# Feature-major products: the high and low parts of x side by side, one matmul of 512 columns for both

## The chip, the core and the metric

One core of a Trainium2 chip runs the whole program once. TensorE (PE) multiplies a stationary tile, loaded by a weight load (PEld), with a moving tile and adds into PSUM; VectorE (DVE), ScalarE (ACT) and GpSimd (POOL) do the element-wise work; SyncE (SP) issues most transfers. Each engine works through its own instructions in the order of the program; semaphores make it wait for the others. The metric is the device time of one execution in microseconds (us), a median over runs.

## What is computed

Two networks in a row on 256 tokens of 1024 features, all in float32. The first has two layers of pooling mixer, stick-breaking attention and a feed-forward part, which is dense SwiGLU in layer 0 and eight experts in layer 1. The second has two layers of a gated recurrence (hgrn), three groups of dilated window attention and a squared-ReLU feed-forward part. Cut to the products that the change touches:

```python
# first block, per layer
proj = h @ w_in[layer]                        # q and k of the stick-breaking attention are columns of proj
f = (silu(h @ ffn_wg) * (h @ ffn_wu)) @ ffn_wd        # layer 0: 2816 hidden columns
# second block, per layer
z = rms_norm(x, norm1_g) @ w_in_2             # zq, zf of the recurrence; q, k of three attention groups
x = x + jnp.square(jax.nn.relu(h2 @ w_up)) @ w_down   # 4096 hidden columns
```

## The kernel before

**Products in three terms.** A float32 operand is kept as a high part (rounded to the type that TensorE multiplies in one pass) and a low part (the rest). x @ w is made of three products, high x high, low x high and high x low, added up in PSUM. `mm3` (line 213) issues the three.

**The weight stream.** Weights come in units of 1 MB, `raw` [128, 2048], loaded by SP. `emit_split` (line 149) makes the high part `whi` on ACT (line 162) and the low part `wlo` on DVE (line 164). All of `raw`, `whi`, `wlo` live in one pool of 13 slots, so the making of a unit's parts can wait for PE to be done with an older unit. `take(1)` hands out the next unit and, first, splits the unit that is two further on: its two instructions stand in the queues of ACT and DVE at that place.

**Token-major products** (`tok_part`, `chunk_tok`, `down`): x is stationary, 512 columns of weights move (lines 221 to 223).

**Feature-major products** (`chunk_feat`): 512 columns of x @ w, turned, so that features lie on partitions. Here a 128 x 128 block of the weights is stationary and the 256 tokens of x move: three matmuls of 256 columns for each block (lines 217 to 219, xh on whi, xl on whi, xh on wlo). A chunk takes two units (j = 0, 1), four column tiles c of 128 features, four k tiles each: 32 triples, 96 matmuls. Two PSUM banks hold the result, two column tiles in each; the pool `acc` has four banks, so two chunks can be in flight. After every second column tile `pump()` emits a piece of the side work (attention, recurrence).

**Consumers.** After a chunk, ACT and DVE read the finished banks, 512 columns at a time: q and k of the mixer (lines 581, 583), SwiGLU in `ffn` (lines 700 to 704: Silu on ACT, product on DVE, high part on ACT, low part on DVE), the gates of the recurrence (lines 1089 to 1099), q and k of the attention groups (line 1117, ACT alone), the squared ReLU of the up-projection (lines 1172 to 1176: Relu on ACT, product on DVE, high part on ACT, low part on DVE). There are 44 chunks: 4 in the mixers, 10 in `ffn`, 16 in the attention stage of the second block, 14 in its two up-projections. `rotate` (line 1217) turns the first 32 rows of q and k on DVE (lines 1219, 1220), with a product on POOL of what a transfer (`rot`) brought.

The order on every engine is that in which the program emits its instructions; nothing reorders them.

Of the kernel before, what the change touches and what calls it, by code (L numbers as in the profile page):

```python
# [43 lines left out]
def constants():  # L44
    """Arrays that follow from the shapes alone."""
# [49 lines left out]
class Net:  # L95
# [81 lines left out]
    def filler(self, n=1):  # L177
        """Work put off to where VectorE would wait."""
# [3 lines left out]
    def ahead(self, split, dma):  # L182
        """Splits the units up to split after the next, loads those up to dma after it."""
# [44 lines left out]
    def tok_part(self, x, ws, t):  # L228
        """Token tile t of 512 columns of x @ w (8 k tiles, two units)."""
# [41 lines left out]
    def chunk_feat(self, x):  # L271
        """Feature-major 512 columns of x @ w: two banks of two 128-column tiles by 256 tokens."""
        xh, xl = x
        out = [self.bank(), self.bank()]
        for j in range(2):
            w = self.take(1)[0]
            for c in range(4):
                o = out[c // 2][:, (c % 2) * T:(c % 2 + 1) * T]
                for k in range(4):
                    kt = 4 * j + k  # L280
                    self.mm3(o, xh[:, kt, :], xl[:, kt, :], w[0][:, k, c * P:(c + 1) * P],
                             w[1][:, k, c * P:(c + 1) * P], kt == 0 and c % 2 == 0, kt == 7,
                             w_stationary=True, skip_group_check=True)
                if c % 2 == 1:
                    self.pump()
        return out

    def down(self, x, nkt, tail=2, done=None, head=None, next_head=None):
        """Token-major x @ w of 1024 columns, 2 k tiles a unit: banks [token tile][half]. The last units
        go tile by tile, and done(t) follows; with head, which makes token tile t of x, all (four)  # L290
        do, and next_head() makes token tile 0 of what comes next while the other's products run."""
# [5 lines left out]
        def part(t, js, ws):  # L297
            """Adds units js to token tile t, half by half."""
# [57 lines left out]
    def to_feat(self, dst, src, t, kt0=0, n=8):  # L356
        """Token-major src [128, n * 128] of token tile t to feature-major high and low parts."""
# [4 lines left out]
    def rstd(self, var, eps, between=None):  # L362
        """(var[0] + var[1] + eps) ** -0.5; between() follows while VectorE would wait."""
# [7 lines left out]
    def load_rows(self, aps, queue=None):  # L371
        """Rows of 1024 on all partitions."""
# [21 lines left out]
        # -mean / 32 and -mean; squares of (x - mean) / 32 add up to the variance.  # L394
# [14 lines left out]
    def rms_norm(self, dst, src, g, acc=None):  # L409
        """dst = norm(src); with acc, src grows by it first."""  # L410
# [13 lines left out]
    def run(self, stop=None):  # L424
# [4 lines left out]
        self.x = (self.main.tile([P, KT, T], F32R, name="xh"), self.main.tile([P, KT, T], F32R, name="xl"))  # L429
# [132 lines left out]
    def mixer(self, l, ps):  # L562
# [3 lines left out]
        with self.mixs:  # L566
# [12 lines left out]
            for j in range(2):  # L579
                ps = self.chunk_feat(self.x)  # L580
                nc.scalar.activation(q[:, 2 * j:2 * j + 2].rearrange("p c t -> p (c t)"), ps[0], AF.Identity,
                                     scale=0.125)
                nc.vector.tensor_copy(k[:, 2 * j:2 * j + 2].rearrange("p c t -> p (c t)"), ps[1])
# [96 lines left out]
    def ffn(self, ps):  # L680
        nc, a, tc = self.nc, self.a, self.tc
        with tc.tile_pool(name="ffn", bufs=1) as pool, tc.tile_pool(name="ffnw", bufs=2) as work:
# [13 lines left out]
            self.side.append(first())  # L696
            for j in range(1, FF // 256):
                ps2 = self.chunk_feat(self.x)
                s = work.tile([P, 512], F32, name="s")
                nc.scalar.activation(s, ps2[0], AF.Silu)  # L700
                nc.vector.tensor_mul(s, s, ps2[1])
                h, l = (m[:, 2 * j:2 * j + 2].rearrange("p c t -> p (c t)") for m in hid)
                nc.scalar.activation(h, s, AF.Identity)
# [691 lines left out]
```

## Time and profile before

| what | value |
|---|---|
| median of 3 runs | 2160.26 us (2159.03 to 2164.56) |
| span of the profiled execution | 2159.9 us |
| PE busy, PEld busy | 98%, 84% of the span |
| DVE busy, ACT busy, POOL busy | 69%, 56%, 4% |
| weights moved | 509 MB, 236 GB/s on average |

The profiled execution's only time of its own is its span; it lies 0.4 us under the median of the runs. The profile lists the busy time of each engine, rows of single instructions (start, duration, what they waited for) and groups of like instructions. Matmuls are pipelined: PE rows overlap, so the pace is the distance between two starts and not the duration in the row. A stretch of `ffn` runs from about 124 to 240 us, the two up-projections from 1513 to 1594 and 1982 to 2063 us, the attention stages from 1223 to 1460 and 1692 to 1930 us, the experts from 430 to 1195 us.

### The profile page before, as it was taken

What the parts mean: (1) busy time and instruction counts of PE and PEld (TensorE: products, weight loads), DVE (VectorE), ACT (ScalarE), POOL (GpSimd) and SP (SyncE); (2) the same over time, 40 slices, a digit from 0 to 9 for tenths busy, and PEclk for the clock granted to TensorE, in tenths of its full rate; (3) what the DMA queues carried; (4) which work ended last, traced back from release to release, by engine and by line L of the source; (5) the groups of instructions that cost most, each with busy time, mean ns of one, the idle gap of its engine ahead of it and who ended that gap; (6) DMA issues with size and microseconds to landing.
All of it is one profiled execution on the core that took longest, in us unless ns stands there. A gap on an engine that the chain in (4) does not pass through costs nothing. (4 is left out here: it accounts for less than half of the span.)

```text
span 2159.9 us, 28622 instructions
## 1 busy us (share of the span) xinstructions
PE 2112.7 (98%) x11787; PEld 1824.0 (84%) x11787; DVE 1498.4 (69%) x1327; ACT 1217.8 (56%) x1199; POOL 81.0 (4%) x91
## 2 busy tenths in 40 slices
PE   7999999999999999999999799999999999999998
PEld 6889978788888888888888599987998899988986
DVE  6465564698888989898989566666654566666643
ACT  4544345677777777777777444464543434455542
POOL 1000000000000000000000101100000011100000
PEclk9999999899999999999999899999999999999999
DMA  9275555599999999999998454444654654436551
GB/s 317 78 234 178 193 169 201 198 362 357 363 338 369 360 343 352 370 363 338 364 353 303 139 181 139 144 157 139 232 195 138 220 165 156 139 123 226 183 194 59
DMA packets 240122, 509.33 MB, mean 236 GB/s; under 512 B 9360, under 2 KB 56592, under 8 KB 239984
## 3 DMA queue, kind: packets, MB, share of 16 engines
q1 hardware_dynamic: 236448, 496.21, 66.6%
q0 software_dynamic: 3248, 10.69, 1.7%
q8 instruction: 95, 1.56, 0.3%
q10 hardware_dynamic: 288, 0.52, 0.1%
q14 instruction: 43, 0.35, 0.0%
HBM read 504.77 MB, written 1.05 MB: 234 GB/s over the span
## 5 line engine op out<-in xcount | busy, mean ns | idle before, releaser
L164 DVE TENSOR_TENSOR wlo<-raw,whi 128x2048 fp32r<-128x2048 f32 x463 | 1062.7, 2298 | 369.1 <-ACT whi L162 313.9
L162 ACT ACTIVATE whi<-raw 128x2048 fp32r<-128x2048 f32 x467 | 886.7, 1914 | 269.0 <-PE acc L222 84.6
L221 PE MATMUL acc<-whi,xh 128*128 128x512 f32 x1168 | 468.0, 401 | 3.1 <-ACT xh L346 2.1
L223 PE MATMUL acc<-whi,xl 128*128 128x512 f32 x1168 | 459.6, 393 | 0.5 <-DVE xl L347 0.5
L222 PE MATMUL acc<-wlo,xh 128*128 128x512 f32 x1168 | 457.5, 392 | 1.6 <-DVE wlo L159 1.0
L217 PE MATMUL acc<-xh,whi 128*128 128x256 f32 x1408 | 404.0, 287 | 0.0
L219 PE MATMUL acc<-xh,wlo 128*128 128x256 f32 x1408 | 398.5, 283 | 0.0
L218 PE MATMUL acc<-xl,whi 128*128 128x256 f32 x1408 | 398.3, 283 | 0.0
L221 PE MATMUL acc<-whi,hidh 128*128 128x512 f32 x696 | 275.9, 396 | 0.0
L223 PE MATMUL acc<-whi,hidl 128*128 128x512 f32 x696 | 275.0, 395 | 0.0
L222 PE MATMUL acc<-wlo,hidh 128*128 128x512 f32 x696 | 274.7, 395 | 0.0
L217 PEld LDWEIGHTS acc<-xh,whi 128*128 128x128 f32 x1408 | 270.0, 192 | 1.3
L218 PEld LDWEIGHTS acc<-xl,whi 128*128 128x128 f32 x1408 | 270.0, 192 | 0.7
L219 PEld LDWEIGHTS acc<-xh,wlo 128*128 128x128 f32 x1408 | 269.9, 192 | 0.2 <-DVE wlo L164 0.2
L223 PEld LDWEIGHTS acc<-whi,xl 128*128 128x128 f32 x1168 | 220.1, 188 | 52.5 <-DVE xl L347 5.9
L221 PEld LDWEIGHTS acc<-whi,xh 128*128 128x128 f32 x1168 | 220.8, 189 | 49.9 <-ACT xh L346 5.5
L222 PEld LDWEIGHTS acc<-wlo,xh 128*128 128x128 f32 x1168 | 221.0, 189 | 46.5 <-DVE wlo L159 1.8
L223 PEld LDWEIGHTS acc<-whi,hidl 128*128 128x128 f32 x696 | 130.9, 188 | 30.9
L222 PEld LDWEIGHTS acc<-wlo,hidh 128*128 128x128 f32 x696 | 131.0, 188 | 29.2
L221 PEld LDWEIGHTS acc<-whi,hidh 128*128 128x128 f32 x696 | 130.9, 188 | 29.1
L346 ACT ACTIVATE xh<-tr 128x512 fp32r<-128x512 f32 x40 | 22.5, 596 | 74.1 <-PE tr L353 73.9
L925 ACT ACTIVATE hidh<-tr 128x512 fp32r<-128x512 f32 (+1 forms) x48 | 27.1, 564 | 64.7 <-PE tr L353 64.7
(305 smaller groups left out, 1603.6 us busy)
## 6 DMA issues: line engine op xcount, KB each, us to landing
raw<-in_moe_wd_dram SPq DMA_DIRECT2D x88, 1024.0 KB, 6.5
raw<-in_moe_wg_dram SPq DMA_DIRECT2D x80, 1024.0 KB, 6.2
raw<-in_moe_wu_dram SPq DMA_DIRECT2D x80, 1024.0 KB, 6.3
raw<-in_w_in_dram SPq DMA_DIRECT2D x74, 1024.0 KB, 5.4
raw<-in_w_up_dram SPq DMA_DIRECT2D x32, 1024.0 KB, 5.4
raw<-in_w_down_dram SPq DMA_DIRECT2D x32, 1024.0 KB, 5.0
raw<-in_w_out_dram SPq DMA_DIRECT2D x16, 1024.0 KB, 5.5
raw<-in_ffn_wg_dram SPq DMA_DIRECT2D x22, 512.0 KB, 4.2
```

The source lines that it names most:

```text
L162: self.nc.scalar.activation(hi, raw, AF.Identity)
L164: self.nc.vector.tensor_sub(lo, raw, hi.bitcast(F32))
L217: mm(out, wh, xh, start=start, stop=False, **kw)
L218: mm(out, wh, xl, start=False, stop=False, **kw)
L219: mm(out, wl, xh, start=False, stop=stop, **kw)
L221: mm(out, xh, wh, start=start, stop=False, **kw)
L222: mm(out, xh, wl, start=False, stop=False, **kw)
L223: mm(out, xl, wh, start=False, stop=stop, **kw)
L346: self.nc.scalar.activation(h, v, AF.Identity)
L925: nc.scalar.activation(h[:, :n], v, AF.Identity)
```

## The change

The high and low parts of x become one tile `xx` [128, 8, 2, 256], high and low of a k tile next to each other. `chunk_feat` then issues two matmuls for each block of weights in place of three: one of 512 columns (high block with both parts of x) and one of 256 (low block with the high part). The first fills both halves of a bank, the second adds into the right half (`out[c][:, T:]`). A column tile thus takes a whole bank, a chunk all four, and the result is the sum of a bank's two halves. The consumers, now functions `sink(c, ...)` called after each column tile, make that sum: ACT copies one half to SBUF, DVE adds the other. They work on 256 columns at a time. The first piece of the side work `first()` is emitted before the first chunk, so that the banks which it reads come free.

```diff
-        self.x = (self.main.tile([P, KT, T], F32R, name="xh"), self.main.tile([P, KT, T], F32R, name="xl"))
+        self.xx = self.main.tile([P, KT, 2, T], F32R, name="xx")
+        self.x = (self.xx[:, :, 0], self.xx[:, :, 1])
...
-    def chunk_feat(self, x):
-        xh, xl = x
-        out = [self.bank(), self.bank()]
+    def chunk_feat(self, sink):
+        mm = self.nc.tensor.matmul
+        out = []
         for j in range(2):
             w = self.take(1)[0]
             for c in range(4):
-                o = out[c // 2][:, (c % 2) * T:(c % 2 + 1) * T]
+                if j == 0:
+                    out.append(self.bank())
                 for k in range(4):
                     kt = 4 * j + k
-                    self.mm3(o, xh[:, kt, :], xl[:, kt, :], w[0][:, k, c * P:(c + 1) * P],
-                             w[1][:, k, c * P:(c + 1) * P], kt == 0 and c % 2 == 0, kt == 7,
-                             w_stationary=True, skip_group_check=True)
+                    cw = slice(c * P, (c + 1) * P)
+                    mm(out[c], w[0][:, k, cw], self.xx[:, kt].rearrange("p i t -> p (i t)"), start=kt == 0, stop=False,
+                       skip_group_check=True)
+                    mm(out[c][:, T:], w[1][:, k, cw], self.xx[:, kt, 0], start=False, stop=kt == 7,
+                       skip_group_check=True)
+                if j == 1:
+                    sink(c, (out[c][:, :T], out[c][:, T:]))
                 if c % 2 == 1:
                     self.pump()
-        return out
...
+                def sink(c, ps, j=j):
+                    if c < 2:
+                        d = q[:, 2 * j + c]
+                        nc.scalar.activation(d, ps[0], AF.Identity, scale=0.125)
+                        nc.vector.scalar_tensor_tensor(d, ps[1], 0.125, d, op0=OP.mult, op1=OP.add)
+                    else:
+                        d = k[:, 2 * j + c - 2]
+                        nc.scalar.activation(d, ps[0], AF.Identity)
+                        nc.vector.tensor_add(d, d, ps[1])
...
+                def sink(c, ps, j=j, gs=gs, us=us):
+                    s = us[:, c - 2] if c > 1 else gs[:, c]
+                    nc.scalar.activation(s, ps[0], AF.Identity)
+                    nc.vector.tensor_add(s, s, ps[1])
+                    if c < 2:
+                        nc.scalar.activation(s, s, AF.Silu)
+                    else:
+                        h, l = (m[:, 2 * j + c - 2] for m in hid)
+                        nc.vector.tensor_mul(s, s, gs[:, c - 2])
+                        nc.scalar.activation(h, s, AF.Identity)
+                        nc.vector.tensor_sub(l, s, h.bitcast(F32))
...
+            def joined(dst, ps):
+                nc.scalar.activation(dst, ps[0], AF.Identity)
+                nc.vector.tensor_add(dst, dst, ps[1])
...
+                    def sink(c, ps, i=i, x=x):
+                        if i == 1 and c == 3:
+                            self.rotate(*qk[0], rope)
+                        joined(x[:, c], ps)
...
-                ps2 = self.chunk_feat(self.x)
-                for i in range(2):
-                    s = work.tile([P, 512], F32, name="s")
-                    nc.scalar.activation(s, ps2[i], AF.Relu)
-                    nc.vector.tensor_mul(s, s, ps2[i])
-                    h, lo = (m[:, 4 * j + 2 * i:4 * j + 2 * i + 2].rearrange("p c t -> p (c t)") for m in hid)
-                    nc.scalar.activation(h, s, AF.Identity)
-                    nc.vector.tensor_sub(lo, s, h.bitcast(F32))
+                def sink(c, ps, j=j):
+                    v = work.tile([P, T], F32, name="s2", bufs=3)
+                    joined(v, ps)
+                    nc.vector.scalar_tensor_tensor(v, v, 0.0, v, op0=OP.max, op1=OP.mult)
+                    h, lo = (m[:, 4 * j + c] for m in hid)
+                    nc.scalar.activation(h, v, AF.Identity)
+                    nc.vector.tensor_sub(lo, v, h.bitcast(F32))
```

The gates of the recurrence have sinks of the same kind (copy and sum, then the sigmoids and products as before).

DVE in the up-projection, one chunk and the two splits ahead of it and behind it, before (`s` is the squared ReLU of 512 columns, `wlo` the low part of a unit):

```order
L164 TENSOR_TENSOR wlo<-raw,whi 128x2048 x2
L1173 TENSOR_TENSOR s<-s,acc 128x512
L1176 TENSOR_TENSOR hidl<-s,hidh 128x512
L1173 TENSOR_TENSOR s<-s,acc 128x512
L1176 TENSOR_TENSOR hidl<-s,hidh 128x512
```

The same place now, the last three column tiles of a chunk and the next splits (the numbered `s` are the tiles named `s2`, one for each column tile):

```order
L1114 TENSOR_TENSOR s_14633<-s_14633,acc 128x256
L1209 SCALAR_TENSOR_TENSOR s_14633<-s_14633 128x256
L1212 TENSOR_TENSOR hidl<-s_14633,hidh 128x256
L1114 TENSOR_TENSOR s_14647<-s_14647,acc 128x256
L1209 SCALAR_TENSOR_TENSOR s_14647<-s_14647 128x256
L1212 TENSOR_TENSOR hidl<-s_14647,hidh 128x256
L1114 TENSOR_TENSOR s_14661<-s_14661,acc 128x256
L1209 SCALAR_TENSOR_TENSOR s_14661<-s_14661 128x256
L1212 TENSOR_TENSOR hidl<-s_14661,hidh 128x256
L164 TENSOR_TENSOR wlo<-raw,whi 128x2048 x2
```

Between two pairs of splits stand twelve instructions of 256 columns where four of 512 stood.

ACT in the same place, before:

```order
L162 ACTIVATE whi<-raw 128x2048 x2
L1172 ACTIVATE s<-acc 128x512
L1175 ACTIVATE hidh<-s 128x512
L1172 ACTIVATE s<-acc 128x512
L1175 ACTIVATE hidh<-s 128x512
```

and now, one whole chunk and the splits behind it:

```order
L1113 ACTIVATE s_14723<-acc 128x256
L1211 ACTIVATE hidh<-s_14723 128x256
L1113 ACTIVATE s_14737<-acc 128x256
L1211 ACTIVATE hidh<-s_14737 128x256
L1113 ACTIVATE s_14751<-acc 128x256
L1211 ACTIVATE hidh<-s_14751 128x256
L1113 ACTIVATE s_14765<-acc 128x256
L1211 ACTIVATE hidh<-s_14765 128x256
L162 ACTIVATE whi<-raw 128x2048 x2
```

A copy (line 1113) and a high part (line 1211) alternate, column tile by column tile, and the next two splits stand behind the last high part.

DVE in the first attention group, at the end of the chunk of k (A, B, D belong to the recurrence, `qa` and `ka` are q and k), before:

```order
L1257 TENSOR_TENSOR A<-A,C 128x512
L1258 TENSOR_TENSOR B<-B,C 128x512
L1261 TENSOR_TENSOR D<-C 128x512
L1219 TENSOR_TENSOR qa<-qa,rope 32x1024
L1220 TENSOR_TENSOR qa<-qa,rot 32x1024
L164 TENSOR_TENSOR wlo<-raw,whi 128x2048
```

and now:

```order
L1114 TENSOR_TENSOR ka<-ka,acc 128x256 x2
L1295 TENSOR_TENSOR A<-A,C 128x512
L1296 TENSOR_TENSOR B<-B,C 128x512
L1299 TENSOR_TENSOR D<-C 128x512
L1114 TENSOR_TENSOR ka<-ka,acc 128x256
L1257 TENSOR_TENSOR qa<-qa,rope 32x1024
L1258 TENSOR_TENSOR qa<-qa,rot 32x1024
L1114 TENSOR_TENSOR ka<-ka,acc 128x256
L164 TENSOR_TENSOR wlo<-raw,whi 128x2048
```

Four sums of 256 columns stand among the work that was there.

## Rows read from the trace of the kernel before

**Rows 1.** The page: busy us, share and instructions; granted clock in 40 slices.
```profile
PE 2112.7 (98%) x11787; PEld 1824.0 (84%) x11787; DVE 1498.4 (69%) x1327; ACT 1217.8 (56%) x1199; POOL 81.0 (4%) x91
...
PEclk9999999899999999999999899999999999999999
```

**Rows 2.** Windows: stretch and length, busy us by engine, clock, DMA share.
```profile
124.00:240.00 116.00, 116.00 (x956) 115.41 (x955) 62.45 (x44) 52.45 (x44) 1.10 (x2) 1.00 0.65 208
1514.00:1594.00 80.00, 80.00 (x670) 80.00 (x669) 50.72 (x43) 40.87 (x41) 0.00 (x0) 1.00 0.62 213
...
1759.00:1783.00 24.00, 23.36 (x123) 19.66 (x122) 18.29 (x20) 11.31 (x16) 5.50 (x3) 1.00 0.53 166
1348.00:1372.00 24.00, 24.00 (x161) 21.95 (x160) 16.53 (x23) 10.89 (x18) 3.50 (x3) 1.00 0.47 140
```

**Rows 3.** Groups by line, PE: out<-in, shape, count | busy us, mean ns.
```profile
L217 PE MATMUL acc<-xh,whi 128*128 128x256 f32 x1408 | 404.0, 287 | 0.0
```

**Rows 4.** Timeline of PE in an up-projection: start us, us, instruction.
```profile
1539.09 0.28 PE L219 MATMUL acc<-xh,wlo 128*128 128x256 f32 x1
1539.21 0.28 PE L217 MATMUL acc<-xh,whi 128*128 128x256 f32 x1
1539.33 0.28 PE L218 MATMUL acc<-xl,whi 128*128 128x256 f32 x1
1539.45 0.28 PE L219 MATMUL acc<-xh,wlo 128*128 128x256 f32 x1
```

**Rows 5.** Timeline of PE in the experts: 512 moving columns.
```profile
440.70 0.39 PE L222 MATMUL acc<-wlo,xh 128*128 128x512 f32 x1
...
442.06 0.39 PE L222 MATMUL acc<-wlo,xh 128*128 128x512 f32 x1
```

**Rows 6.** Timeline of PE in the dense down-projection: 512 moving columns.
```profile
250.15 0.39 PE L222 MATMUL acc<-wlo,hidh 128*128 128x512 f32 x1
...
257.12 0.40 PE L222 MATMUL acc<-wlo,hidh 128*128 128x512 f32 x1
```

**Rows 7.** Timeline of ACT in an up-projection: [idle before, what ended it].
```profile
1536.95 0.60 ACT L1172 ACTIVATE s<-acc 128x512 f32<-128x512 f32 x1 [0.27 <-PE acc L219]
1538.31 0.63 ACT L1175 ACTIVATE hidh<-s 128x512 fp32r<-128x512 f32 x1 [0.75 <-DVE s L1173]
1538.84 1.90 ACT L162 ACTIVATE whi<-raw 128x2048 fp32r<-128x2048 f32 x1
1542.65 1.91 ACT L162 ACTIVATE whi<-raw 128x2048 fp32r<-128x2048 f32 x1 [1.91 <-PE acc L219]
...
1548.47 0.60 ACT L1172 ACTIVATE s<-acc 128x512 f32<-128x512 f32 x1 [0.32 <-PE acc L219]
```

**Rows 8.** Timeline of DVE in the same place.
```profile
1540.77 2.29 DVE L164 TENSOR_TENSOR wlo<-raw,whi 128x2048 fp32r<-128x2048 f32 x1 [1.11 <-ACT whi L162]
1544.59 2.29 DVE L164 TENSOR_TENSOR wlo<-raw,whi 128x2048 fp32r<-128x2048 f32 x1 [1.53 <-ACT whi L162]
1546.81 0.68 DVE L1173 TENSOR_TENSOR s<-s,acc 128x512 f32<-128x512 f32 x1
```

**Rows 9.** Groups by line, ACT: PSUM to SBUF of 256 and 512, SBUF to SBUF.
```profile
L1175 ACT ACTIVATE hidh<-s 128x512 fp32r<-128x512 f32 x28 | 17.7, 632 | 30.8 <-DVE s L1173 30.8
...
L649 ACT ACTIVATE mixh<-ms 128x256 fp32r<-128x256 f32 x8 | 3.1, 384 | 9.6 <-PE ms L647 9.6
```

**Rows 10.** Groups by line, DVE, of 256 columns.
```profile
L677 DVE SCALAR_TENSOR_TENSOR mixl<-tr,psc,mixh 128x256 fp32r<-128x256 f32 x8 | 3.9, 484 | 10.4 <-ACT mixh L676 10.4
...
L1353 DVE TENSOR_TENSOR oa<-oa,ms 128x256 f32<-128x256 f32 x8 | 3.4, 422 | 8.4 <-PE ms L1347 8.0
...
L1352 DVE TENSOR_TENSOR oa<-oa,w 128x256 f32<-128x256 f32 x8 | 3.3, 415 | 0.0
```

**Rows 11.** Chain of waits, in order of time: start us, us, in the second attention stage.
```profile
1762.59 3.68 DMA rot<-ka
...
1768.64 3.34 DVE ka L1219
```

More of the change, by code (lines that the diff above doesn't have):

```diff
@@ L694, in first @@
                     self.split_to(hid, self.transpose4(hs[t], 2), 0, t, 2)
-            self.side.append(first())
+            f = first()
+            next(f)
+            self.side.append(f)
             for j in range(1, FF // 256):
-                ps2 = self.chunk_feat(self.x)
-                s = work.tile([P, 512], F32, name="s")
-                nc.scalar.activation(s, ps2[0], AF.Silu)
-                nc.vector.tensor_mul(s, s, ps2[1])
-                h, l = (m[:, 2 * j:2 * j + 2].rearrange("p c t -> p (c t)") for m in hid)
-                nc.scalar.activation(h, s, AF.Identity)
-                nc.vector.tensor_sub(l, s, h.bitcast(F32))
+                gs, us = (work.tile([P, 2, T], F32, name=n) for n in ("s", "u"))
+                def sink(c, ps, j=j, gs=gs, us=us):
[9 more added lines that the diff above has]
+                        nc.vector.tensor_sub(l, s, h.bitcast(F32))
+                self.chunk_feat(sink)
                 if j == 6:
@@ L866, in gather @@
                                    skip_group_check=True)
[L867 removed]
+                        nc.scalar.activation(xg[i][:, k:k + 2], ps.rearrange("p (k s) -> p k s", k=2), AF.Identity)
             def turn(p):
@@ L1085, in second, with sink @@
             f = pool.tile([P, 4 * T], F32, name="C")
-            ps = self.chunk_feat(self.x)
-            for i in range(2):
-                c = slice(512 * i, 512 * i + 512)
-                nc.scalar.activation(f[:, c], ps[i], AF.Sigmoid)
-                nc.scalar.activation(k[:, c], ps[i], AF.Sigmoid, scale=-1.0)
-            for h in range(4):
+            og = pool.tile([P, 2, 512], F32, name="og")
+            def joined(dst, ps):
+                nc.scalar.activation(dst, ps[0], AF.Identity)
+                nc.vector.tensor_add(dst, dst, ps[1])
+            def sink(h, ps):
                 c = slice(T * h, T * h + T)
+                joined(f[:, c], ps)
+                nc.scalar.activation(k[:, c], f[:, c], AF.Sigmoid, scale=-1.0)
+                nc.scalar.activation(f[:, c], f[:, c], AF.Sigmoid)
                 nc.vector.tensor_scalar(f[:, c], f[:, c], lb[:, 4 + h:5 + h], lb[:, h:h + 1], op0=OP.mult, op1=OP.add)
                 nc.vector.tensor_scalar(k[:, c], k[:, c], lb[:, 4 + h:5 + h], None, op0=OP.mult)
-            ps = self.chunk_feat(self.x)
-            for i in range(2):
-                c = slice(512 * i, 512 * i + 512)
-                nc.scalar.activation(q[:, c], ps[i], AF.Sigmoid)
-                nc.vector.tensor_mul(q[:, c], q[:, c], ps[i])
-            og = pool.tile([P, 2, 512], F32, name="og")
+            self.chunk_feat(sink)
+            def sink(h, ps):
+                c = slice(T * h, T * h + T)
+                s = og[:, h // 2, h % 2 * T:h % 2 * T + T]
+                joined(q[:, c], ps)
+                nc.scalar.activation(s, q[:, c], AF.Sigmoid)
+                nc.vector.tensor_mul(q[:, c], q[:, c], s)
+            self.chunk_feat(sink)
             ps = self.chunk_tok(self.x)
@@ L1111, in second @@
                 for i in range(2):
-                    ps = self.chunk_feat(self.x)
-                    if i == 1:
-                        self.rotate(*qk[0], rope)
                     x = pool.tile([P, 4, T], F32, name="qa" if i == 0 else "ka", bufs=2)
-                    for j in range(2):
-                        nc.scalar.activation(x[:, 2 * j:2 * j + 2].rearrange("p c t -> p (c t)"), ps[j], AF.Identity)
+                    def sink(c, ps, i=i, x=x):
+                        if i == 1 and c == 3:
+                            self.rotate(*qk[0], rope)
+                        joined(x[:, c], ps)
+                    self.chunk_feat(sink)
                     rot = pool.tile([32, 4, T], F32, name="rot")
@@ L1165, in first @@
                     self.split_to(hid, self.transpose4(hs[t]), 0, t)
-            self.side.append(first())
+            f = first()
+            next(f)
+            self.side.append(f)
             for j in range(1, FF2 // 512):
-                ps2 = self.chunk_feat(self.x)
-                for i in range(2):
-                    s = work.tile([P, 512], F32, name="s")
-                    nc.scalar.activation(s, ps2[i], AF.Relu)
-                    nc.vector.tensor_mul(s, s, ps2[i])
-                    h, lo = (m[:, 4 * j + 2 * i:4 * j + 2 * i + 2].rearrange("p c t -> p (c t)") for m in hid)
-                    nc.scalar.activation(h, s, AF.Identity)
-                    nc.vector.tensor_sub(lo, s, h.bitcast(F32))
+                def sink(c, ps, j=j):
[5 more added lines that the diff above has]
+                    nc.vector.tensor_sub(lo, v, h.bitcast(F32))
+                self.chunk_feat(sink)
             acc3 = self.down(hid, FF2 // P)
```

6 lines of the change are left out of this document (1 added, 5 removed).

## The prediction

> **What bounds the kernel now.** I read the page first: PE is busy 98% of the span, at a full granted clock in nearly every slice [rows 1]. Busy PE alone says little, so next the windows by stage. In the dense feed-forward part and in the up-projections PE has no gap and PEld is busy throughout as well, while DVE is busy for 54% and 63% and ACT for 45% and 51% [rows 2]. So PE's own pace sets these stages. The timeline gives that pace: feature-major matmuls of 256 columns start 120 ns apart, a triple in 360 ns [rows 4]; there are 1408 triples [rows 3], 32 in each of 44 chunks, 11.52 us a chunk. Matmuls of 512 columns start 226.7 ns apart in the experts (1.36 us for six) [rows 5] and 232.3 in the dense down-projection (6.97 us for thirty) [rows 6]. Both are under twice 120: a matmul has a fixed part of 8 to 13 ns, and that is what the change can save.
>
> Last I read ACT and DVE beside one up-projection chunk, since their order changes most. A chunk's end shows as the Relu that waits for PE: 1536.95, then 1548.47, which is 11.52 us [rows 7]. Between these stand two splits. The first `whi` starts at 1538.84 right behind the chunk's last high part; its `wlo` follows 0.03 us after it. The second `whi` starts at 1542.65, released by PE half-way through the next chunk, and its `wlo` ends at 1546.88 [rows 7, 8]. DVE then takes up the consumers with 0.07 us of overlap [rows 8]. So the two engines go round a ring (last high part, whi, wlo, whi, wlo, consumers) once in a chunk, and wait for PE at two places in it: 1.91 us before the second `whi`, 0.32 before the Relu [rows 7]. What the change adds to the ring meets that slack first.
>
> **PE's side.** A triple becomes 512 + 256 columns: 226.7 to 232.3 plus 120 ns, 347 to 352. I take 348, the experts' pace, with 1 ns to spare, since these stages are as evenly fed: 12 ns saved on a triple, 0.38 us on a chunk (11.14 us), 16.9 us on all 1408. Bounds: 8 and 13.3 ns, 11 and 19 us. The Trainium skill (TensorE: Matmul & The Clock Gate, Back-to-back issue gap) gives N/2.4 + 2.5 ns, by which the triple would go from 327.5 to 325.0 ns and all of them save 3.5 us. The trace disagrees with it on both sizes, 120 for 109 and 227 to 232 for 216; the sum goes by the rows.
>
> **The consumers' side.** Every column tile now has its own bank, copied by ACT and added to by DVE, 256 columns at a time. ACT takes 0.384 us for 256 columns out of PSUM; from SBUF 512 take 0.632 [rows 9] and 2048 take 1.90 [rows 7], 0.83 ns a column, so 256 about 0.42. DVE takes 0.415 to 0.42 for a sum or difference of 256 [rows 10]. The squared ReLU in one instruction has no row; its nearest are 0.415 (two tensors) and 0.484 (with a scalar operand) [rows 10]; I take 0.45 and keep both ends.
>
> *Up-projections (14 chunks).* Per column tile the queues hold: sum on DVE 0.42, product 0.45 (0.02 behind it), high part on ACT 0.42, low part on DVE 0.42, each crossing 0.03, less the 0.07 of overlap: 1.72 us. They do not run beside each other: ACT's next copy stands behind this tile's high part, and DVE's next sum behind this tile's low part. From the end of `wlo`: three tiles 5.16, the fourth up to its high part 1.34, less 0.07, is 6.43. Then `whi` 1.81 (1.90 less 0.09 of overlap), `wlo` 0.03 + 2.29, second `wlo` 2.22; the second `whi` runs beside the first `wlo`. The ring: 6.43 + 1.81 + 2.32 + 2.22 = 12.8 us, against 11.14 of PE. With the ends of the product's price and 0.1 us a tile for the crossings it is 12.4 to 13.2. So here the ring takes PE's place: with four banks, PE can't begin a chunk's tile c before DVE has added up tile c of the chunk before, and what is queued behind that sum on DVE are the next weights' low parts.
>
> The start has some credit. From a stage's first matmul the first chunk's second `whi` waits for PE half-way, 5.57, then 1.91 + 0.03 + 2.29 + 0.35 to the end of the first sum: 10.15 us, one microsecond before PE needs the bank. The seventh chunk's first sum ends 6 x 12.8 later, at 86.9; its fourth tile's 5.2 later, at 92.1. The down-projection's first unit (24 matmuls, 5.57 us) needs that bank for its last six, 1.39 us, and ends at 93.5, as if it had begun at 87.9. Before it began at 7 x 11.52 = 80.6. **+7.3 us a layer, +14.6 in two** (bounds +9 and +20). The down-projection can't give it back: it is PE's own time [rows 6].
>
> *Dense feed-forward part (10 chunks).* By the same rows: sum 0.35, Silu 0.44, copy 0.30, sum 0.45, Silu 0.44, copy 0.29, sum 0.45, product 0.44, high part 0.45, low part 0.45, sum 0.35, product 0.44, high part 0.45: 5.30, and 6.35 for the splits, 11.65 us. Ten chunks: 10.15 + 9 x 11.65 = 115.0, before 115.2. **0 us** (-3 to +4): the ring eats PE's gain.
>
> *Attention stages and mixers (20 chunks).* A tile's copy and sum have no ring of their own, as a rule: ACT's copies don't wait for DVE. Four sums, 1.7 us a chunk, go onto a DVE that is busy 69% in a stretch of the first stage and 76% in one of the second [rows 2]; a bank's sum has 4.2 us (three tiles of PE's next use) before PE waits. So PE's gain stays: 20 x 0.38 = -7.7. Against it: in the first group of the second attention stage the chain already leaves PE, over the transfer of `rot` for k (3.68 us) and the rotation (3.34) [rows 11]. That transfer waits for q's rotation to give up its buffer, and four sums now stand ahead of this in DVE's queue. In the first stage the same place has a few microseconds to spare. I put +3 us for these (0 to +20, below). **-5 us.** The moved `first()` costs nothing: its copies stand ahead of the same splits that they followed, and PE reaches the third bank only 2.8 us later.
>
> **Sum.** The profiled span is 2159.9, 0.4 under the median. +14.6 + 0 - 7.7 + 3 = +9.9: a span near 2169.8, a median of **2170 us**, 0.45% slower. What a measurement of this kernel can tell from no change is about 0.3%, 6.5 us: 2153.8 to 2166.7.
>
> **Rivals.**
> *A. The ring sets the up-projections*, as worked out: 2170. For it: the order of the queues is fixed and every duration has a row near it.
> *B. PE still sets every stage.* Then the whole 16.9 us is saved: **2143 us**, faster. For it: PEld is busy all the time in these stages [rows 2] and loses a third of its loads; DVE would be busy 9.7 us of 11.14 and ACT 7.0, neither of them all the time. It decides at a ring under 11.14 us, which needs column tiles of 1.3 us; 1.72 is far from that unless the low part gives way to the next sum. The Trainium skill (Perfetto Trace Analysis, Identifying the Most-Contended Engine) would read it so: the busiest engine is the one to improve, and for TensorE the share of weight loads counts. The windows agree on which is busiest; they don't show that two half-idle engines wait for each other in turn.
> *C. A shorter ring.* With tiles of 1.55 us the ring is 12.3, the up-projections +3.7 a layer, the feed-forward part -2: 7.5 - 2 - 7.7 = -2, **2158 us**, no difference.
> *D. The attention stages lose too.* If DVE's queue there can't take the sums without holding PE's banks, each of the 12 chunks of q and k puts up to 1.7 us on PE's path, 20 in place of 3: **2187 us**. It decides where a sum falls behind a wait of DVE for an exponential or for `rot` by more than 4.2 us. Against it: 24 to 31% of DVE's time there is idle [rows 2].
> *E. The wide matmul gives nothing*, 240 ns for 512 columns: the ring is the same and the 7.7 us are missing: **2178 us**. Against it [rows 5, 6].
>
> **How the numbers follow.** A 0.55, B 0.10, C 0.18, D 0.12, E 0.05. Faster is B: 0.10. No difference is C and the lowest 0.02 of A: 0.20. Slower is the rest: 0.70. The range leaves out B and the upper half of D: from 2157 (C with a little more stall saved) to 2186, which also holds A with the ring's upper bound (2175) and the feed-forward part's (+4).
>
> **What the changed profile would show.** PE's feature-major starts 227 to 232 and 120 ns apart where it doesn't wait; if 240, E. In the up-projections, chunks some 12.8 us apart, PE with gaps of up to a microsecond before column tiles, released by DVE's sum, and DVE going from low part to sum without idle time; if the chunks are 11.1 apart, B. The feed-forward part near 116 us, as before. In the attention stages the same number of waits of PE; many new ones would be D. The forecast fails above all if a column tile's round of ACT and DVE is not 1.72 us.

## The result and the profile after

The changed kernel takes 2179.59 us (2179.32 to 2181.52, 4 runs), beside 2160.59 us of the kernel before (2159.03 to 2164.56, 4 runs): a ratio of 1.0083 (95% interval 1.0069 to 1.0096), 19 us slower. A second comparison, below, gave 1.0057 (1.0042 to 1.0071), 12 us. Slower, then, as forecast (2170 us, 9.7 over the median shown before it), within the range, and by more than forecast. One execution of the kernel `best`, below, took 2325.48 us at a mean granted clock of 0.845 and is left out of that kernel's figures.

The page of the changed kernel (busy us and share by engine) shows no engine in trouble, beside [rows 1]:

```profile
PE 2119.7 (97%) x10379; PEld 1748.4 (80%) x10379; DVE 1577.3 (72%) x1579; ACT 1249.9 (57%) x1379; POOL 80.5 (4%) x91
```

The windows by stage do more (stretch and length, then busy us by engine, clock, DMA share): the dense feed-forward part and the first up-projection, to be held against the first two of [rows 2].

```profile
128.00:244.00 116.00, 114.61 (x643) 98.14 (x642) 77.00 (x97) 65.22 (x98) 1.10 (x2) 1.00 0.64 207
1518.00:1602.00 84.00, 81.14 (x436) 65.97 (x435) 59.81 (x88) 42.48 (x65) 0.00 (x0) 1.00 0.59 196
```

PE, without a gap there before, now has 1.4 us of them in the feed-forward part and 2.9 in the up-projection; PEld falls from all the time to 79%. DVE is busy for 71% of the up-projection and ACT for 51%: neither is full. The gaps tell less than what was lost: rows of PE overlap, so a start that comes 0.30 us after the one before it, where 0.12 is the pace, shows as 0.02 us of idle time (at 1542.21 us).

Where the time went is read from PE's starts: the distance from the first feature-major matmul of a stage to that of the next, in us (differences are taken before rounding). Two pairs of profiles are shown, since the start differs from profile to profile (the two on the right are from the second comparison).

| from ... to | before | after | difference | before | after | difference |
|---|---|---|---|---|---|---|
| start to first chunk | 31.4 | 36.0 | +4.7 | 32.6 | 32.4 | -0.2 |
| first mixer | 96.0 | 95.3 | -0.7 | 95.7 | 95.3 | -0.4 |
| dense feed-forward part, to second mixer | 191.6 | 192.3 | +0.6 | 191.7 | 192.3 | +0.7 |
| second mixer and experts | 910.8 | 908.9 | -1.9 | 909.2 | 909.7 | +0.5 |
| recurrence and attention, layer 0 | 283.0 | 283.9 | +0.9 | 283.0 | 283.7 | +0.7 |
| up- and down-projection, layer 0 | 185.0 | 192.9 | +7.9 | 185.0 | 193.0 | +8.0 |
| recurrence and attention, layer 1 | 283.9 | 283.9 | 0.0 | 283.5 | 282.9 | -0.5 |
| up-projection to last matmul, layer 1 | 170.5 | 178.8 | +8.3 | 170.5 | 178.5 | +8.0 |
| sum | 2152.2 | 2172.1 | +19.8 | 2151.1 | 2167.9 | +16.8 |

The up-projections carry 16 of it in both pairs. Next the round of DVE and ACT there, one chunk, which stands in the place of [rows 7] and [rows 8]. DVE (start us, us, instruction, idle before it and what ended that; L1114 is the sum, L1209 the product, L1212 the low part):

```profile
1537.84 2.29 DVE L164 TENSOR_TENSOR wlo<-raw,whi 128x2048 fp32r<-128x2048 f32 x1
1540.05 0.41 DVE L1114 TENSOR_TENSOR s<-s,acc 128x256 f32<-128x256 f32 x1
1540.49 0.42 DVE L1209 SCALAR_TENSOR_TENSOR s<-s 128x256 f32<-128x256 f32 x1
1541.40 0.42 DVE L1212 TENSOR_TENSOR hidl<-s,hidh 128x256 fp32r<-128x256 f32 x1 [0.48 <-ACT hidh L1211]
1541.74 0.41 DVE L1114 TENSOR_TENSOR s<-s,acc 128x256 f32<-128x256 f32 x1
...
1546.50 0.43 DVE L1212 TENSOR_TENSOR hidl<-s,hidh 128x256 fp32r<-128x256 f32 x1 [0.48 <-ACT hidh L1211]
1548.31 4.68 DVE L164 TENSOR_TENSOR wlo<-raw,whi 128x2048 fp32r<-128x2048 f32 x2 [1.38 <-ACT whi L162]
1552.90 0.41 DVE L1114 TENSOR_TENSOR s<-s,acc 128x256 f32<-128x256 f32 x1
```

ACT in the same place:

```profile
1546.05 0.42 ACT L1211 ACTIVATE hidh<-s 128x256 fp32r<-128x256 f32 x1 [1.01 <-DVE s L1209]
1546.37 3.71 ACT L162 ACTIVATE whi<-raw 128x2048 fp32r<-128x2048 f32 x2
1549.98 0.36 ACT L1113 ACTIVATE s<-acc 128x256 f32<-128x256 f32 x1
1553.80 0.42 ACT L1211 ACTIVATE hidh<-s 128x256 fp32r<-128x256 f32 x1 [3.46 <-DVE s L1209]
```

A column tile's round is 1541.74 - 1540.05 = 1.69 us, of which DVE sits 0.48 us idle for the high part on ACT; ACT in its turn waits 1.01 us for DVE's product. From the first sum of a chunk to the next it is 1552.90 - 1540.05 = 12.85 us. What PE makes of it, in the same chunk (PE, one column tile's end and the next one's start):

```profile
1551.96 0.39 PE L285 MATMUL acc<-xx,whi 128*128 128x512 f32 x1
1552.19 0.28 PE L287 MATMUL acc<-xx,wlo 128*128 128x256 f32 x1
1552.31 0.39 PE L285 MATMUL acc<-xx,whi 128*128 128x512 f32 x1
1552.54 0.28 PE L287 MATMUL acc<-xx,wlo 128*128 128x256 f32 x1
1553.37 0.50 PE L285 MATMUL acc<-xx,whi 128*128 128x512 f32 x1 [0.55 <-DVE s L1114]
1553.71 0.28 PE L287 MATMUL acc<-xx,wlo 128*128 128x256 f32 x1
```

Where it doesn't wait, PE goes 0.23 us from the wide to the narrow matmul and 0.12 back, a pair in 0.347 to 0.350 us where the triple took 0.360 [rows 4]. Then it stands still for the sum that gives up its bank: the instruction that starts at 1552.90 in the row of DVE ends just before PE starts at 1553.37. The chain of waits through this stretch (1518 to 1606 us) is that ring, by its shares:

```profile
by line: DVE wlo L164 33.9%; ACT whi L162 15.2%; DVE s L1209 12.4%; DVE s L1114 9.7%; ACT hidh L1211 9.4%; DVE hidl L1212 9.2%; issue 4.4%; PE acc L285 3.1%; PE acc L287 1.6%; PE tr L359 1.0%; DVEq L164 0.2%
```

PE's three lines have under 6% of it, in a stage where it had been the bound.

### The profile page after: what moved, and what is told of

Same layout as the page of the kernel before. It is cut to its first block, busy times and chain, and to the rows that moved or that the text cites. A ratio compares the mean times of both kernels' runs of the same rounds, so it can differ in the third digit from the quotient of the medians.

```text
span 2179.7 us, 26238 instructions
## 1 busy us (share of the span) xinstructions
PE 2119.7 (97%) x10379; PEld 1748.4 (80%) x10379; DVE 1577.3 (72%) x1579; ACT 1249.9 (57%) x1379; POOL 80.5 (4%) x91
## 5 line engine op out<-in xcount | busy, mean ns | idle before, releaser
L285 PE MATMUL acc<-xx,whi 128*128 128x512 f32 x1408 | 509.7, 404 | 7.1 <-DVE s L1114 4.8
L221 PE MATMUL acc<-whi,xx 128*128 128x512 f32 x1168 | 470.0, 402 | 4.8 <-ACT whi L158 2.9
L223 PE MATMUL acc<-whi,xx 128*128 128x512 f32 x1168 | 461.7, 395 | 0.5 <-DVE xx L353 0.5
L222 PE MATMUL acc<-wlo,xx 128*128 128x512 f32 x1168 | 459.6, 393 | 1.8 <-DVE wlo L159 1.2
L287 PE MATMUL acc<-xx,wlo 128*128 128x256 f32 x1408 | 394.6, 280 | 0.0
L285 PEld LDWEIGHTS acc<-xx,whi 128*128 128x128 f32 x1408 | 264.9, 188 | 81.7 <-DVE s L1114 19.1
L287 PEld LDWEIGHTS acc<-xx,wlo 128*128 128x128 f32 x1408 | 266.3, 189 | 0.7
L221 PEld LDWEIGHTS acc<-whi,xx 128*128 128x128 f32 x1168 | 221.8, 190 | 52.6 <-ACT xx L352 5.3
L223 PEld LDWEIGHTS acc<-whi,xx 128*128 128x128 f32 x1168 | 221.2, 189 | 52.6 <-DVE xx L353 5.9
L222 PEld LDWEIGHTS acc<-wlo,xx 128*128 128x128 f32 x1168 | 221.8, 190 | 46.8 <-DVE wlo L159 2.0
L1211 ACT ACTIVATE hidh<-s 128x256 fp32r<-128x256 f32 x56 | 23.4, 418 | 89.6 <-DVE s L1209 89.6
L1212 DVE TENSOR_TENSOR hidl<-s,hidh 128x256 fp32r<-128x256 f32 x56 | 23.8, 425 | 27.1 <-ACT hidh L1211 27.1
```

The source lines that it names most:

```text
L221: mm(out, xh, wh, start=start, stop=False, **kw)
L222: mm(out, xh, wl, start=False, stop=False, **kw)
L223: mm(out, xl, wh, start=False, stop=stop, **kw)
L285: mm(out[c], w[0][:, k, cw], self.xx[:, kt].rearrange("p i t -> p (i t)"), start=kt == 0, stop=False, skip_group_check=True)
L287: mm(out[c][:, T:], w[1][:, k, cw], self.xx[:, kt, 0], start=False, stop=kt == 7, skip_group_check=True)
L1211: nc.scalar.activation(h, v, AF.Identity)
```

## The experiments

Two questions were open: whether the ring is the cause, or only what stands beside it; and where the other microseconds are (the start, the attention). The stages of the runs, in us and as in the table above:

| kernel | start | feed-forward part | attention 0 | up/down 0 | attention 1 | up to end, 1 |
|---|---|---|---|---|---|---|
| before | 31.4 | 191.6 | 283.0 | 185.0 | 283.9 | 170.5 |
| after | 36.0 | 192.3 | 283.9 | 192.9 | 283.9 | 178.8 |
| up_old | 35.8 | 192.2 | 283.8 | 185.0 | 282.8 | 170.5 |
| up_behind | 35.4 | 192.5 | 283.8 | 182.1 | 284.1 | 167.6 |
| att_nosum | 36.3 | 192.2 | 281.8 | 192.9 | 281.9 | 178.4 |
| layout | 30.1 | 191.6 | 283.1 | 185.0 | 283.9 | 170.5 |
| behind | 35.1 | 189.3 | 283.6 | 182.1 | 282.8 | 167.6 |
| best | 36.8 | 189.0 | 282.6 | 182.1 | 282.6 | 167.6 |

### up_old: the up-projections as before

```diff
-                def sink(c, ps, j=j):
...
-                self.chunk_feat(sink)
+                ps2 = self.chunk_old(self.x)      # three matmuls of 256 columns, two banks
+                for i in range(2):
+                    s = work.tile([P, 512], F32, name="s")
+                    nc.scalar.activation(s, ps2[i], AF.Relu)
...
```

> The changed kernel with the old chunks and consumers (three matmuls of 256 columns, two banks, 512 columns at a time) in the two up-projections alone. Theory A (there the ring of ACT and DVE sets the pace): a chunk takes 11.52 us again in place of the 12.86 read from the changed kernel, the two up-projections and the first unit of their down-projections give back 2 x 8 us, a median near 2164 us (2162 to 2166). Rival (the ring is a symptom, and the loss comes from what the whole kernel pays, clock or transfers): at most 5 us come back, 2175 or more.

Measured: 2162.69 us (2157.77 to 2165.61, 10 runs), the kernel before beside it 2164.65 (20 runs), a ratio of 0.9991 (0.9979 to 1.0002). The stage is 185.0 and 170.5 us again, to the tenth. The loss of the change sits in these two stages whole; all its other places together come to nothing that can be measured (the interval runs from 4.5 us faster to 0.4 slower).

### up_behind: the same instructions in another order

```diff
                 def sink(c, ps, j=j):
                     v = work.tile([P, T], F32, name="s2", bufs=3)
-                    joined(v, ps)
-                    nc.vector.scalar_tensor_tensor(v, v, 0.0, v, op0=OP.max, op1=OP.mult)
                     h, lo = (m[:, 4 * j + c] for m in hid)
-                    nc.scalar.activation(h, v, AF.Identity)
-                    nc.vector.tensor_sub(lo, v, h.bitcast(F32))
+                    nc.scalar.activation(v, ps[0], AF.Identity)
+                    if behind:
+                        behind[0]()               # product and high part of the tile before
+                    nc.vector.tensor_add(v, v, ps[1])
+                    if behind:
+                        behind[1]()               # low part of the tile before
...
+                    behind[:] = high, lambda: nc.vector.tensor_sub(lo, v, h.bitcast(F32))
```

> The changed kernel with the same instructions, in another order, in the up-projections: product, high part and low part of a column tile stand one tile later, so that DVE goes product(c-1), sum(c), low(c-1) and ACT copy(c), high(c-1), with nothing to wait for in a tile. Theory A (the order makes the ring): a tile's round falls from 1.70 us to the DVE time alone, 0.43 + 0.41 + 0.42 = 1.27, the ring to 4 x 1.27 + 1.5 (whi behind the last high part) + 4.6 (two wlo) = 11.2 us, about PE's own 11.14; chunks some 11.2 us apart, 2 x 9 us less, near 2161 us (2157 to 2165). Rival (the number of consumer instructions, or traffic on PSUM and SBUF, holds PE up, whatever their order): chunks stay near 12.8 us and the time near 2179.

Measured: 2157.64 us (2155.36 to 2158.86, 5 runs), a ratio to the kernel before of 0.9966 (0.9952 to 0.9980): from 0.8% slower to 0.3% faster, with as many instructions on each engine as in the changed kernel (PE 10379, DVE 1579, ACT 1379). DVE in an up-projection of this kernel (L1213 sum, L1218 product, L1221 low part), two tiles and the passage to the next chunk:

```profile
1550.84 0.42 DVE L1218 SCALAR_TENSOR_TENSOR s<-s 128x256 f32<-128x256 f32 x1
1551.18 0.42 DVE L1213 TENSOR_TENSOR s<-s,acc 128x256 f32<-128x256 f32 x1
1551.74 0.42 DVE L1221 TENSOR_TENSOR hidl<-s,hidh 128x256 fp32r<-128x256 f32 x1 [0.15 <-ACT hidh L1219]
1552.09 0.42 DVE L1218 SCALAR_TENSOR_TENSOR s<-s 128x256 f32<-128x256 f32 x1
1552.42 0.41 DVE L1213 TENSOR_TENSOR s<-s,acc 128x256 f32<-128x256 f32 x1
1552.99 0.42 DVE L1221 TENSOR_TENSOR hidl<-s,hidh 128x256 fp32r<-128x256 f32 x1 [0.15 <-ACT hidh L1219]
1554.80 4.74 DVE L164 TENSOR_TENSOR wlo<-raw,whi 128x2048 fp32r<-128x2048 f32 x2 [1.38 <-ACT whi L162]
1559.45 0.42 DVE L1218 SCALAR_TENSOR_TENSOR s<-s 128x256 f32<-128x256 f32 x1
```

A tile's round is 1.24 us in place of 1.69: DVE's wait for the high part has fallen from 0.48 to 0.15 us, since the next tile's sum stands in it. In the window of this stretch PE is back at all the time:

```profile
1517.00:1593.00 76.00, 76.00 (x443) 67.12 (x442) 59.45 (x88) 42.82 (x64) 0.00 (x0) 1.00 0.67 222
```

Seven chunks take 78.46 us from the first start to the last, against 87.72 in the changed kernel and 81.38 before: 11.21 a chunk, PE's own pace of 0.350 us a pair. DVE has 88 instructions in either window, of 59.45 us here and 59.81 above. That a wait for the order, not the amount of work, was the cause is thus shown; the rival that the number of instructions holds PE up has fallen.

### att_nosum: no sums for q and k of the attention

```diff
-                        joined(x[:, c], ps)
+                        nc.scalar.activation(x[:, c], ps[0], AF.Identity)
```

> The changed kernel without the sum of a bank's two halves for q and k of the attention groups (48 sums of 0.41 us on DVE in two layers' six pairs of chunks; the low part of x is left out of q and k there). Theory (these sums push the recurrence and the window attention on DVE back, and PE waits for them later, 1.1 us at a time, three times in a layer): those waits go and PE's gain in the 12 chunks is kept, 4 to 6 us less, near 2175 us. Rival (the waits come from PE arriving earlier at work that DVE ends no earlier, sums or not): two thirds of them stay and it is 2178 us or more.

The kernel leaves out what stands in the second half of these banks: both products with a low part, of x or of the weights, for q and k.

Measured: 2177.35 us (2174.94 to 2178.96, 4 runs), a ratio of 1.0058 (1.0041 to 1.0075), the kernel before at 2164.65. Against the changed kernel's two ratios (1.0083, 1.0057) that tells little; the stages tell it: 2.0 us less in either layer than in the changed kernel's first profile, 1.9 and 1.0 less than in its second. PE's waits from 1255 to 1515 us in the changed kernel (total us, times, longest):

```profile
PE tr L359 <- DVE y L1328: 0.8, 1, 0.8
PE ms L1285 <- DVE B L1296: 0.7, 1, 0.7
PE tr L359 <- ACT p L1367: 0.7, 1, 0.7
PE acc L221 <- ACT xx L352: 0.6, 2, 0.3
PE tr L359 <- DVE oa L1396: 0.4, 1, 0.4
PE acc L223 <- DVE xx L353: 0.2, 1, 0.2
```

The same in att_nosum:

```profile
PE acc L221 <- ACT xx L352: 0.6, 2, 0.3
PE tr L359 <- DVE oa L1396: 0.4, 1, 0.4
PE tr L359 <- ACT p L1367: 0.3, 1, 0.3
PE acc L223 <- DVE xx L353: 0.2, 1, 0.2
PE tr L359 <- DVE y L1328: 0.2, 1, 0.2
```

The first three are new in this layer, and all are PE's at side work (the recurrence's state product at L1285, two transposes of its and the attention's results), none at a bank of q or k. Without the sums one is gone and the other two lose 0.6 and 0.4 us. They were expected to go; 0.5 us of 2.2 stays. So the sums are behind most of it, but not by their length alone. In front of two of the three waits stands an instruction of DVE that ran at the same time as POOL's product for `rot` and took some 2 us longer than usual: the rotation of k ahead of the state product, and a step of the softmax on 128x2 numbers ahead of the second transpose (POOL and DVE in the changed kernel):

```profile
1301.11 3.33 POOL L1256 TENSOR_TENSOR rot<-rot,rope 32x1024 f32<-32x1024 f32 x1 [2.88 <-DMA rot<-ka]
1302.12 3.40 DVE L1257 TENSOR_TENSOR ka<-ka,rope 32x1024 f32<-32x1024 f32 x1
1406.08 2.39 POOL L1256 TENSOR_TENSOR rot<-rot,rope 32x1024 f32<-32x1024 f32 x1 [2.14 <-DMA rot<-ka]
1406.60 1.89 DVE L1359 TENSOR_SCALAR w<-w 128x2 f32<-128x2 f32 x1
```

and the rotation of k in att_nosum, after POOL's product:

```profile
1298.66 2.38 POOL L1256 TENSOR_TENSOR rot<-rot,rope 32x1024 f32<-32x1024 f32 x1 [2.59 <-DMA rot<-ka]
1303.12 1.21 DVE L1257 TENSOR_TENSOR ka<-ka,rope 32x1024 f32<-32x1024 f32 x1
```

The step of the softmax takes 0.17 us at this place in the kernel before and 1.90 in att_nosum too, where that wait keeps 0.3 us. In the first group's place the ten profiles of this document have twenty rotations of k. Nine start while POOL's product runs; they take 3.39 to 3.43 us and end 1.08 us behind its end, and behind each of them PE waits 0.6 to 0.8 us at the state product. Eleven take 1.20 or 1.21 us, and PE waits there once, 0.2 us. In layer 0 all five profiles with the sums of q and k have this meeting, and none of the five without them. In layer 1 it comes and goes, in the kernel before as well (0.6 us of wait in its first profile), so the wait isn't new there. With it go the two lengths of attention 1 with these sums: 283.9 and 284.1 us where the two meet, 282.8 to 282.9 where they don't.

### layout, after_again, before_again: the start

`layout` is the kernel before with `xx` in place of `xh` and `xl`; beside this only one copy in the experts is written with another view of the same data.

> The kernel before with nothing but the new place of x: the high and low parts side by side in one tile. In the profile of the changed kernel the start, up to the first chunk, takes 4.7 us longer with the granted clock at half between 20 and 31 us, though no instruction there is other than before but for this layout. Theory (the start differs by chance of clock and transfers from run to run): 2160 us (2157 to 2163). Rival (the layout slows the reading of x at the start or everywhere): 2163 us or more, with the longer start in its profile.

Measured: 2162.31 us (2159.85 to 2165.34, 10 runs), a ratio of 0.9992 (0.9983 to 1.0002), and a start of 30.1 us. The place of x in SBUF costs nothing that can be measured.

The other two are the two kernels unaltered.

> The changed kernel, unaltered, beside the kernel before once more, since runs of the kernel before lie 8 us apart (2158 to 2167) and its profile and that of the change differ by 4.7 us ahead of the first feature-major chunk. Theory (the start is chance: an earlier or a later landing of the second weight unit, and half the clock after it, in either kernel): the change is 15 us slower than the kernel before on the same chip, a ratio near 1.007, and some of its profiles start as the one of before did. Rival (the longer start belongs to the change): 19 us, 1.009, as in the first comparison.

> The kernel before, unaltered, for a second profile of its start. Theory of chance: the first chunk may start at 31 us or at 35 us, with the granted clock at half between 20 and 31 us in the second case. Rival: it starts at 30 to 32 us with full clock again, as in both profiles with old chunks in the first mixer, where all four with the new ones show 35 to 36 us.

Measured: the changed kernel 2176.20 us (2175.05 to 2177.35, 4 runs) beside 2164.35 of the kernel before (11 runs), a ratio of 1.0057 (1.0042 to 1.0071); the kernel before 2160.55 in its one run. The changed kernel's first chunk starts at 32.4 us this time, 36.0 the first time. Windows of its start in the first profile (busy us by engine, granted clock):

```profile
20.00:25.00 5.00, 2.82 (x6) 1.70 (x6) 2.50 (x5) 1.86 (x4) 0.56 (x1) 0.58 1.14 287
25.00:30.00 5.00, 4.54 (x15) 3.33 (x14) 2.25 (x4) 0.60 (x1) 0.00 (x0) 0.50 1.09 348
```

and in the second:

```profile
20.00:25.00 5.00, 2.89 (x9) 1.72 (x8) 2.85 (x5) 1.06 (x1) 0.56 (x1) 0.85 1.13 286
25.00:30.00 5.00, 5.00 (x23) 4.00 (x22) 2.17 (x3) 3.00 (x3) 0.00 (x0) 0.81 1.09 349
```

In the first, the half of the second weight unit that `whi` waits for landed 2.5 us later (ACT took it up at 18.33, in the second at 15.88), PE's two next matmuls came 1.8 and 1.3 us after the ones before them (1.4 and 0.8 us of it idle), and PE then worked at a granted clock of 0.50, the lower of its two levels (1.2 GHz), through 25 to 30 us. The second has idle times of the same length before 21.69 and 22.95 us and some 3 us at the lower level, the first some 10. The same program shows both, so the change's instructions don't bring the late start every time; `layout` speaks against the layout. What stays open is whether the change makes the late landing more frequent: the three profiles with old chunks in the first mixer start at 30.1 to 32.6 us, and of seven with new ones six at 35.1 to 36.8. The runs of the kernel before, 2158 to 2167 us in twenty, are as wide as this.

### behind and best: what the change can give

`behind` puts the consumers one column tile behind in the feed-forward part too; `best` takes the old chunks back for q and k of the attention groups.

```diff
+                    if behind:
+                        behind[0]()               # product and high part of the tile before
                     nc.vector.tensor_add(s, s, ps[1])
+                    if behind:
+                        behind[1]()               # Silu, or the low part, of the tile before
                     if c < 2:
-                        nc.scalar.activation(s, s, AF.Silu)
...
+                        behind[:] = lambda: None, lambda: nc.scalar.activation(s, s, AF.Silu)
...
```

> The changed kernel with the consumers one column tile behind in the up-projections (as in the run before this) and in the dense feed-forward part too. If the ring of ACT and DVE took PE's gain in the feed-forward part (11.65 us a chunk against 11.14 of PE), its ten chunks take 112 us in place of 115.6, and the kernel 4 us less than with the up-projections alone: 2153.5 us where that gave 2157.6. If PE's own pace sets 115.6 there, no difference: 2157.6.

Measured: 2154.68 us (2154.42 to 2155.78, 5 runs), a ratio to the kernel before of 0.9960 (0.9947 to 0.9973). The ten chunks take 112.86 us from first start to last, 115.6 in the changed kernel: 2.7 us less, where 3.6 were expected. PE has no gap over 0.05 us there any more, so 11.29 us a chunk is its own pace, 0.353 us a pair with the side work in it. The ring had taken PE's gain in this part, as forecast; the gain is smaller than forecast.

> The same, and q and k of the attention groups by the old chunks (three matmuls of 256 columns, no sums on DVE). Theory (there the sums cost as much as PE gains: three waits of PE of about 1 us at side work in a layer): the stage from the first chunk of the recurrence to the first up-projection chunk takes 283.0 us less 0.8 for the recurrence's two chunks, in place of 283.9, 1.7 us a layer; 3.5 us less in all than without it, near 2150 us. Rival (the waits come from elsewhere, PE's gain of 0.38 us a chunk is lost): 0 to 4 us more than without it.

Measured: a ratio of 0.9943 (0.9930 to 0.9956), 2149.5 to 2154.6 us in the runs compared: 12 us faster than the kernel before. The two attention stages are 282.6 us both; the first is 1.0 us shorter than in `behind` and the second 0.2, less than the 1.7 expected; the first is the layer in which `behind` has k's rotation beside POOL's product, the second the one in which it hasn't. PE's waits from 1263 to 1513 us:

```profile
PE acc L221 <- ACT xx L368: 0.6, 2, 0.3
PE tr L375 <- DVE oa L1432: 0.4, 1, 0.4
PE acc L223 <- DVE xx L369: 0.3, 1, 0.3
```

The three new waits are gone, and these three are the kernel before's in that layer. Against `behind` alone the difference in time (1.2 us by the two stages) is too small to be told by the runs, but its sign is that of the theory: for q and k of the attention the old chunks are no worse.

## Why the prediction was right, and where not

**The ring in the up-projections: right.** Forecast were a tile of 1.72 us, a ring of 12.8, +7.3 us a layer; the trace has 1.69 to 1.70, 12.85, and +7.9 to +8.3. The single prices held: the sum 0.41, the product, which had no row of its own, 0.42 to 0.43 (0.45 taken, and the neighbour with two tensors was the right one [rows 10]), high and low part 0.42 to 0.43. The splits were priced short, 4.68 us for both `wlo` on DVE where 4.51 were put, and the tiles long by half as much, so part of the ring's exactness is luck. Of the 8 us, 6.35 lie between the first and the last start of the chunks (87.72 for 81.38); 1.6 more come in the down-projection's first unit, whose four groups of six matmuls start 1.66 to 1.70 us apart, at the pace of the tiles whose banks they take. The forecast's 7.3 held both.

**Rival B fell.** PE's busy share said that PE would go on setting the pace, and after the change DVE is at 71% and ACT at 51%. The Trainium skill (Perfetto Trace Analysis, Identifying the Most-Contended Engine) looks for the engine that is most used; the trace agrees that this was PE, and neither kernel has a fuller one, yet the stage went to two engines that are idle for 29% and 49% of it. What showed it ahead was the order in the two queues.

**The feed-forward part: right within a microsecond.** Forecast 0, measured +0.6 and +0.7; the starts of `whi` are 11.63 us apart in five rounds and 11.81 in the last three (11.65 forecast).

**The attention stages and mixers: the step that failed.** Forecast -7.7 for PE's gain in 20 chunks and +3 for stalls. The chunks did get shorter, by 2.2 us a layer between their own first and last starts where the forecast has 8 x 0.38 = 3.1. But the stage from the first chunk of the recurrence to the up-projection took +0.9 and +0.7 us in layer 0 and 0.0 and -0.5 in layer 1, and the first mixer gave 0.4 to 0.7. The step read: a tile's copy and sum have no ring of their own, so PE's gain stays. It looked for PE waiting at the banks of q and k, and there it never waits. The stalls came at the side work, where PE asks for what DVE makes behind the sums: 2.2 us at three new places in layer 0 of the first profile. In layer 1 two places are new (0.9 and 0.8 us); the third, 0.8, was 0.6 in the kernel before and is gone in the second profile. With the slower starts behind each stop, PE's path between the chunks grew by 3.0 and 2.2 us in that profile. None of these waits is for the transfer of `rot` itself, on which the 3 us were put, though its landing starts POOL's product. At one place the sums delay DVE by their own length (0.67 of 0.82 us go without them), as D has it in small; at two, DVE meets POOL's product of `rot`. The prediction read the rotation of k at 3.34 us [rows 11] as its price, where it takes 1.21 when it doesn't meet that product, and held that the first stage had a few microseconds to spare at this place; PE waits 0.7 there. D's 20 us were four times too many, A's 3 too few, and the gain to set against them smaller than its 7.7.

**PE's gain: the right pace, a little too large.** Forecast 348 ns a pair for 360; in a run of pairs without a wait 347 to 350. Where no ring is left the stages gave 0.42 us a chunk in the up-projections (81.38 less 78.46, in seven) and 0.26 in the feed-forward part (115.5 less 112.86, in ten) for 0.38 forecast. The Trainium skill's N/2.4 + 2.5 ns (TensorE: Matmul & The Clock Gate, Back-to-back issue gap), which that section calls the gap of an isolated matmul, would put a wide and a narrow one at an estimated 216 + 109 = 325 ns; the trace has 230 + 117.

**The sum.** Forecast +9.9 by terms; the two pairs of profiles have +15.2 and +17.0 from the first chunk on. Up-projections 1.4 to 1.7 over the forecast, feed-forward part 0.6 to 0.7, attention and first mixer 4.5 to 4.9 over it make +17.1 and +16.4; the second mixer with the experts, -1.9 and +0.5 with spells of lower clock in them, is the rest. The rest of the first pair's 19.8, 4.7 us, is the start, which had no term and should have had one in the range: the same kernel's profiles differ there by 4 us. C's sum has no stalls in it, which A's puts at 3; with them it is 2161 and not 2158, and nothing else hangs on it.

## What to carry to other kernels

When a step is moved from one long instruction per chunk to several short ones per tile that go back and forth between two engines, write down the round: each crossing makes both engines wait, and the round's length, times the tiles, plus what else stands in these queues, must be under the pace of the engine that feeds them. If it isn't, don't cut work first: put each tile's later steps one tile behind, so that one engine's wait is filled with the next tile's work (here 1.69 to 1.24 us a tile and, by the stages, 22 us in the two up- and down-projections, without a single instruction less). And a sum added to a busy engine is paid where some other engine waits for the work behind it, so look for the price there and not at the sum's own buffers. And where an instruction takes 3.4 us in one place and 1.2 in another, see what runs beside it before either is taken as its price.

## What the runs showed of the hardware

A wait costs PE more than its length: after one, the next matmul starts 0.33 to 0.34 us after the wide one that waited (1553.37 to 1553.71 above) where without a wait it is 0.23, so some 0.1 us goes at each stop; in the changed up-projections there are four stops a chunk.

DVE and POOL can hold each other up: k's rotation on DVE takes 1.2 us, and 3.4 where it starts during POOL's product of `rot`, ending 1.08 us behind the end of that in each of nine cases; a DVE instruction on 128x2 numbers takes 0.17 us, and 1.89 beside the same product.

The start of one unchanged program differs: the granted clock was 0.50 and 0.81 in the same 5 us of two profiles, with the first chunk 3.6 us later in the first. How much of this the clock costs and how much the later landing of the second weight unit isn't separated, and what brings either isn't shown: the two profiles of the kernel before take up that unit at nearly the same time (16.13 and 16.18 us), and only one of them has the lower clock behind it, for some 3 us.
